# A hybrid decoder layer on one core: low parts of the mixer's weights on VectorE, four more raw weight buffers, and y loaded through GpSimd's queue

## The chip, the core and the metric

The kernel runs on one core of a Trainium2 chip. Its engines work side by side, each through its own instructions in order: TensorE (PE, matmuls; PEld is its loading of weights), VectorE (DVE), ScalarE (ACT), GpSimd (POOL) and SyncE (SP, which here only issues DMA transfers). A transfer is issued by an engine, waits in that engine's order for what it needs, and then lands by itself. The metric is the time of one execution in microseconds of device time, the median of three runs.

## The reference

One layer of a decoder for 512 prompt tokens and 8 samples of 4 tokens, 544 columns in all, with 1024 features in float32:

```python
x = x + 0.5 * SwiGLU_1(RMSNorm(x))          # ffn1: gate and up 1024 x 2816, down 2816 x 1024
z = RMSNorm(x) @ w_in                       # 1024 x 3584, split among the head groups
attn = MoBA(q_a, k_a, v_a)                  # 8 heads of 64, block-sparse attention, paged cache for the samples
rec  = norm(HGRN2(q_b, f_b, i_b)) * silu(g) # 4 heads of 128, gated linear recurrence
x = x + concat(attn, rec) @ w_out           # 1024 x 1024
x = x + 0.5 * SwiGLU_2(RMSNorm(x))          # ffn2, as ffn1
```

It returns the outputs for prompt and samples, the new keys and values, and the states of the recurrence.

## The kernel before

Activations lie transposed: 128 features on the partitions and 544 tokens along the row, worked on in two halves of 272 columns. To come near float32 accuracy each factor is split into a high part (rounded to the short float that a matmul takes at full rate) and a low part (the rest), and each product is three matmuls: high weight with high x, high weight with low x, low weight with high x. The tiles are named so: `whi` and `wlo` are the parts of a weight, `xh` and `xl` those of x.

Three stages follow each other. ffn1 runs until about 402 us, the mixer (w_in, the chains of attention and recurrence, w_out) until about 781 us, ffn2 to the end. A **block** is an output block of 128 features: for w_in (28 blocks) and w_out (8 blocks) it takes two **units** of weights, each 4 x 128 rows by 128 columns (256 KB), and 48 matmuls of 128x272. In the ffn the first NREG = 5 hidden blocks are plain too; from the sixth on the kernel multiplies gate and up in **paired** blocks of seven units, built from five loaded or summed quarters of the weights (a11, a21, their sum, a22, a12), which save a matmul in eight. `xh0..7` and `xl0..7` of the norm's output are the slots that raw weights may use as well once the plain blocks are over; `sq` and `t_g` are copies of partial sums that ScalarE takes out of TensorE's accumulators (`mm` and `sm`) to free them.

Weights pass through two kinds of slots. `w_load` brings a unit from memory into a raw slot (`raw`, four buffers). `w_split` and `split_unit` make the parts in one of six w slots: ScalarE casts `whi`, and then either VectorE subtracts (`wlo = raw - whi`), or ScalarE writes minus the rounded raw into `wlo` in a second pass and GpSimd issues an adding DMA that lays raw onto it (the **transfer**, row `wlo<-raw` of POOL). A raw slot is free when its last reader is done, and that reader is the transfer where there is one. `w_pump` keeps a number of units ahead of TensorE: AHEAD = 4, and AHEAD_MIX = 6 while the job to split is one of the mixer's. Before the change both units of a w_in or w_out block go by transfer; of the ffn's first plain blocks only the second unit does.

The order of all instructions is made by a planner: generators record each instruction with a planned start, computed from costs by shape, and `give_out` (lines 279 to 288) then issues them per engine in the order of planned starts. Nearly every instruction of the profile therefore has line 288, and one goes by tile names. A planned order is fixed: an engine that waits at an instruction holds up whatever is planned behind it.

At the end of the mixer `ffn2` (line 1902) opens its pool on the memory of the mixer's pool, loads the residual `y` (eight tiles of 128 x 544, 272 KB each) from `xspill` (tile name `xs`), and w_out's accumulators are added onto it on VectorE (`y<-mm,y`).

## Time and profile before

| | before |
|---|---|
| runs, us | 1222.38, 1219.51, 1221.71; median 1221.71 |
| profiled execution, us | 1219.56, of which its span 1217.8 |
| PE / PEld busy | 1180.5 (97%) / 1117.7 (92%) |
| DVE / ACT / POOL busy | 780.5 (64%) / 600.8 (49%) / 281.8 (23%) |
| low parts by transfer | 90, 256 KB each, 4.0 us to landing |
| DMA | 177.26 MB, mean 146 GB/s |

The span is what the profile covers; the execution's time is 1.8 us longer. The profile's tables give, for stretches of the span, each engine's busy time, the granted TensorE clock as a share of full speed (PEclk), and the busy share of the DMA engines. In a list of single instructions, the bracket at the end of a line tells how long the engine was idle before it and what ended that.

### The profile page before, as it was taken

To read this page: it belongs to the slowest core of one execution; us is meant where nothing else is said; L and a number is where in the kernel's file an instruction comes from. 1 tells how busy PE (TensorE), PEld (TensorE's weight loads), DVE (VectorE), ACT (ScalarE), POOL (GpSimd) and SP (SyncE) were. 2 spreads that over 40 slices of the span, in tenths; PEclk is the share of its full clock that TensorE was granted. 3 is DMA by queue.
4 is the path that set the end of the run, shared out by engine and by line. 5 is a ranking of instruction groups with operands and counts; after the bars stand their busy time and mean duration, and the time that the engine had idled before them with its cause. 6 is when DMAs were issued, how large, how long until landed. Compare 5 with 4: busy or idle time off the path is not lost.

```text
span 1217.8 us, 26505 instructions
## 1 busy us (share of the span) xinstructions
PE 1180.5 (97%) x10571; PEld 1117.7 (92%) x10571; DVE 780.5 (64%) x1662; ACT 600.8 (49%) x1223; POOL 281.8 (23%) x293
## 2 busy tenths in 40 slices
PE   8999999999999989999999999699989999999998
PEld 8989999999999988889888777599989999999998
DVE  5888458854775377875675357237767478845853
ACT  6645246532555446666556533255544255514642
POOL 4121021101103541213354446141110011101000
PEclk9999999999999989999999999799989999999999
DMA  6566444453325984755787988565455334533232
GB/s 171 130 168 161 127 134 120 124 139 79 87 66 153 223 214 116 174 122 133 225 230 205 277 282 272 124 158 120 118 153 157 86 87 122 142 102 87 53 110 69
DMA packets 234607, 177.26 MB, mean 146 GB/s; under 512 B 14019, under 2 KB 206051, under 8 KB 234484
## 3 DMA queue, kind: packets, MB, share of 16 engines
q1 hardware_dynamic: 206740, 108.83, 30.8%
q0 software_dynamic: 27648, 66.60, 23.8%
q8 instruction: 83, 1.36, 0.5%
q14 instruction: 40, 0.33, 0.1%
q10 hardware_dynamic: 96, 0.14, 0.0%
HBM read 133.94 MB, written 11.83 MB: 120 GB/s over the span
## 4 chain that ended last, share of the span: by engine, by line
PE 85%; DVE 5%; DMA 4%; issue 3%; ACT 1%; POOL 1%; SPq 0%; POOLq 0%; ACTq 0%; DVEq 0%
PE mm L288 58%; PE sm L288 27%; DMA wlo<-raw 1%; DMA raw<-ffn_gate 1%; DMA raw<-w_in 1%; DMA SC<-rsample 0%; DMA xin<-x_prompt 0%; DVE ms_qk L288 0%; DVE wlo L288 0%; DVE xl L288 0%; SPq L288 0%; POOL wlo L288 0%; DVE t_qk L288 0%; ACT sq L288 0%; POOL KV L288 0%
## 5 line engine op out<-in xcount | busy, mean ns | idle before, releaser
L288 PE MATMUL mm<-xh,whi 128*128 128x272 f32 x1216 | 364.5, 300 | 11.1 <-DVE y L288 9.2
L288 PE MATMUL mm<-xl,whi 128*128 128x272 f32 x1216 | 352.6, 290 | 2.0 <-DVE xl L288 1.9
L288 PE MATMUL mm<-xh,wlo 128*128 128x272 f32 x1216 | 352.5, 290 | 0.1
L288 ACT CAST whi<-raw 128x512 fp32r<-128x512 f32 (+1 forms) x256 | 154.5, 606 | 224.5 <-PE mm L288 160.5
L288 PEld LDWEIGHTS mm<-xh,whi 128*128 128x128 f32 x1216 | 231.6, 190 | 26.8 <-issue 13.6
L288 PEld LDWEIGHTS mm<-xl,whi 128*128 128x128 f32 x1216 | 231.3, 190 | 3.1 <-DVE xl L288 3.0
L288 PEld LDWEIGHTS mm<-xh,wlo 128*128 128x128 f32 x1216 | 231.1, 190 | 0.4 <-issue 0.4
L288 DVE TENSOR_TENSOR wlo<-raw,whi 128x512 fp32r<-128x512 f32 (+1 forms) x166 | 113.4, 690 | 61.9 <-ACT whi L288 59.1
L288 PE MATMUL mm<-hw,whi 128*128 128x272 f32 x704 | 132.3, 288 | 0.0
L288 POOL DMA_DIRECT2D wlo<-raw x90 | 81.3, 931 | 218.2 <-ACT wlo L288 181.8
L288 PE MATMUL sm<-xw,whi 128*128 128x272 f32 x648 | 124.3, 290 | 0.4 <-ACT t_g L288 0.4
L288 PE MATMUL mm<-xw,whi 128*128 128x272 f32 x648 | 123.2, 288 | 0.8 <-ACT t_g L288 0.8
L288 PEld LDWEIGHTS mm<-hw,whi 128*128 128x128 f32 x704 | 110.2, 188 | 0.2 <-issue 0.2
L288 PEld LDWEIGHTS sm<-xw,whi 128*128 128x128 f32 x648 | 102.8, 190 | 0.6 <-ACT t_g L288 0.6
L288 PEld LDWEIGHTS mm<-xw,whi 128*128 128x128 f32 x648 | 101.9, 189 | 1.0 <-ACT t_g L288 1.0
L288 PE MATMUL mm<-hw,wlo 128*128 128x272 f32 x352 | 101.2, 287 | 0.0
L288 PE MATMUL sm<-xw,wlo 128*128 128x272 f32 x324 | 94.0, 290 | 0.0
L288 PE MATMUL mm<-xw,wlo 128*128 128x272 f32 x324 | 93.3, 288 | 0.0
L288 PEld LDWEIGHTS mm<-hw,wlo 128*128 128x128 f32 x352 | 66.3, 188 | 0.0
L288 PE MATMUL sm<-xw,xh 128*128 128x272 f32 x304 | 60.6, 295 | 3.0 <-ACT sq L288 3.0
L288 PEld LDWEIGHTS sm<-xw,wlo 128*128 128x128 f32 x324 | 61.7, 190 | 0.2
L288 PE MATMUL mm<-xw,xh 128*128 128x272 f32 x304 | 59.7, 292 | 2.1 <-ACT sq L288 2.1
(324 smaller groups left out, 2163.4 us busy)
## 6 DMA issues: line engine op xcount, KB each, us to landing
wlo<-raw POOLq DMA_DIRECT2D x90, 256.0 KB, 4.0
raw<-ffn_down SPq DMA_DIRECT2D x64, 256.0 KB
raw<-w_in SPq DMA_DIRECT2D x56, 256.0 KB
raw<-ffn_gate SPq DMA_DIRECT2D x38, 256.0 KB
raw<-ffn_up SPq DMA_DIRECT2D x36, 256.0 KB
xl<-ffn_up SPq DMA_DIRECT2D x28, 256.0 KB
xh<-ffn_gate SPq DMA_DIRECT2D x26, 256.0 KB
xh<-ffn_up SPq DMA_DIRECT2D x24, 256.0 KB
```

Of the source, the lines that this page charges most:

```text
L288: call(*map(real, args), **{k: real(v) for k, v in kw.items()})
```

## The change

Of a w_in block only the second unit's low part is now made by a transfer, the first on VectorE; of w_out none is. So 44 of the 90 transfers and as many ScalarE passes go, and VectorE gets 44 subtractions. AHEAD_MIX goes, so four units are kept ahead everywhere. At its start each ffn registers four more raw slots, rawx0 to rawx3, for paired jobs only. The eight loads of y in ffn2 are issued by GpSimd instead of SyncE.

```diff
--- before.py
+++ after.py
@@ -51,8 +51,8 @@
 MIXED = (4, 5, 6, 0, 1, 2, 3, 7)
 OVER, TICK, WARM_COLUMNS = 0.0112, 3.413, 3060
 NREG = 5
+NX = 4
 AHEAD = 4
-AHEAD_MIX = 6
 PACE = 1.1
 WARM = 10
 SLACK = -0.1
@@ -514,12 +514,11 @@
             return [rows[0], rows[1]]
 
         def job(kind, src, nk):
-            out.append({"kind": kind, "src": src, "nk": nk // 2, "raw": [], "done": 0, "paired": kind is not None, "mixer": False})
-
-        def plain(m, nk, r0, c0, mixer=False, start=False):
+            out.append({"kind": kind, "src": src, "nk": nk // 2, "raw": [], "done": 0, "paired": kind is not None})
+
+        def plain(m, nk, r0, c0, transfer=False):
             job(None, quarters(m, nk, r0, c0), nk)
-            out[-1]["mixer"] = mixer
-            out[-1]["start"] = start
+            out[-1]["transfer"] = transfer
 
         def paired(kind, nk, a11, a12, a21, a22, transfer):
             job(kind, [a11, a21, a21 if transfer else None, a22, a12], nk)
@@ -530,8 +529,8 @@
             for g0, ng in FGROUPS[pairs]:
                 for f in range(g0, g0 + ng):
                     if f < NREG:
-                        plain(gate, KD, 0, 128 * f, start=True)
-                        plain(up, KD, 0, 128 * f, start=True)
+                        plain(gate, KD, 0, 128 * f, transfer=True)
+                        plain(up, KD, 0, 128 * f, transfer=True)
                     else:
                         paired("a", KD, *quarters(gate, KD, 0, 128 * f), *quarters(up, KD, 0, 128 * f), pairs)
                 for m in range(0, KD, 2):
@@ -543,9 +542,9 @@
 
         ffn("ffn1", False)
         for n, j in IN_ORDER:
-            plain(a["w_in"][0], KD, 0, COLS[n] + 128 * j, True)
+            plain(a["w_in"][0], KD, 0, COLS[n] + 128 * j, transfer=True)
         for m in range(KD):
-            plain(a["w_out"][0], KD, 0, 128 * m, True)
+            plain(a["w_out"][0], KD, 0, 128 * m)
         ffn("ffn2", False)
         return out
 
@@ -649,7 +648,7 @@
                 job["last"] = self.split_unit(a22, nk, xs[1], job["transfer"])
             drop = {1: (3,), 2: (1,), 4: (2,), 5: (0, 4)}.get(n, ())
         else:
-            self.units.append(self.split_unit(job["raw"][n][0], nk, xs[0], job["mixer"] or n == 1 and job["start"]))
+            self.units.append(self.split_unit(job["raw"][n][0], nk, xs[0], n == 1 and job["transfer"]))
             drop = (n,)
         for i in drop:
             raw, y = job["raw"][i]
@@ -660,11 +659,7 @@
         return True
 
     def w_pump(self):
-        def ahead():
-            mixer = self.splitting < len(self.jobs) and self.jobs[self.splitting]["mixer"]
-            return len(self.units) < (AHEAD_MIX if mixer else AHEAD)
-
-        while (ahead() and self.w_split()) or self.w_load():
+        while (len(self.units) < AHEAD and self.w_split()) or self.w_load():
             pass
 
     def next_w(self, n):
@@ -960,6 +955,7 @@
     def ffn(self, pool, wide, home, x, xg, done, pairs, first=None):
         nc = self.nc
         self.pairs, self.sums, self.hidden_raw = pairs, wide, (pool, "t_h")
+        self.more_slots("a", wide, [f"rawx{i}" for i in range(NX)], [])
         for g0, ng in FGROUPS[pairs]:
             last = g0 + ng == NFF
             hs = []
@@ -1904,7 +1900,7 @@
         with self.pool("ffn2") as pool:
             x = [pool.tile([128, T], F32, name=f"y{k}") for k in range(KD)]
             for k in range(KD):
-                nc.sync.dma_start(x[k], xspill[k])
+                nc.gpsimd.dma_start(x[k], xspill[k])
             xg = []
             for m in range(KD):
```

Where the instructions stand, at three places. First SyncE at the end of w_out, before the change (`raw` are weight buffers, `y<-xs` the residual's loads):

```order
L288 DMA raw_10682<-w_out 128x4x128
L288 DMA raw_10684<-w_out 128x4x128
L288 DMA raw_10686<-w_out 128x4x128
L288 DMA raw_10688<-w_out 128x4x128
L288 DMA y_10694<-xs_57 128x544
L288 DMA y_10696<-xs_58 128x544
L288 DMA y_10698<-xs_59 128x544
L288 DMA y_10700<-xs_60 128x544
L288 DMA y_10702<-xs_61 128x544
L288 DMA y_10704<-xs_62 128x544
L288 DMA y_10706<-xs_63 128x544
L288 DMA y_10708<-xs_64 128x544
```

The same place after the change, still SyncE:

```order
L288 DMA raw_10542<-w_out 128x4x128
L288 DMA raw_10608<-w_out 128x4x128
L288 DMA raw_10626<-w_out 128x4x128
L288 DMA rawx_2092_10646<-ffn_gate 128x4x128
L288 DMA rawx_2093_10648<-ffn_up 128x4x128
L288 DMA rawx_2095_10650<-ffn_up 128x4x128
L288 DMA raw_10671<-w_out 128x4x128
L288 DMA raw_10681<-w_out 128x4x128
L288 DMA raw_10802<-w_out 128x4x128
L288 DMA raw_10809<-w_out 128x4x128
```

The y loads are gone from SyncE, and three loads of ffn2's weights into the new slots stand among those of w_out. On GpSimd at that place before (s is the recurrence's state, sqsum the norm's sum of squares):

```order
L288 TENSOR_TENSOR s_1802_9139<-s_1802_9139,hf_9130 128x512
L288 TENSOR_TENSOR s_1803_9171<-s_1803_9171,hf_9130 128x512
L288 DMA wlo_10634<-raw_10125 128x512
L288 DMA wlo_10651<-raw_10158 128x512
L288 DMA wlo_10674<-raw_10455 128x512
L288 DMA wlo_10679<-raw_10471 128x512
L288 TENSOR_TENSOR sqsum_10731<-sqsum_10731,sq_1923_10745 128x544
```

and after:

```order
L288 TENSOR_TENSOR s_1796_9089<-s_1796_9089,hf_9198 128x512
L288 TENSOR_TENSOR s_1797_9137<-s_1797_9137,hf_9198 128x512
L288 DMA y_10644<-xs_57 128x544
L288 DMA y_10652<-xs_58 128x544
L288 DMA y_10654<-xs_59 128x544
L288 DMA y_10665<-xs_60 128x544
L288 DMA y_10683<-xs_61 128x544
L288 DMA y_10698<-xs_62 128x544
L288 DMA y_10718<-xs_63 128x544
L288 DMA y_10735<-xs_64 128x544
L288 TENSOR_TENSOR sqsum_10710<-sqsum_10710,sq_1917_10737 128x544
```

The four transfers of w_out went and the eight y loads stand where they were.

Second, the first paired block of ffn2. SyncE before, from the loads of that block on (raw are the four raw buffers, xh and xl the norm's slots used for raw weights):

```order
L288 DMA xl_2139_11958<-ffn_up 128x4x128
L288 DMA raw_11960<-ffn_gate 128x4x128
L288 DMA xh_2138_11963<-ffn_gate 128x4x128
L288 DMA xl_2141_11967<-ffn_up 128x4x128
L288 DMA xl_2250_11975<-ffn_gate 128x4x128
L288 DMA xh_2142_11978<-ffn_gate 128x4x128
L288 DMA raw_11994<-ffn_gate 128x4x128
L288 DMA raw_12018<-ffn_down 128x4x128
```

and after:

```order
L288 DMA raw_11731<-ffn_gate 128x4x128
L288 DMA raw_11744<-ffn_gate 128x4x128
L288 DMA raw_11804<-ffn_up 128x4x128
L288 DMA rawx_2127_11878<-ffn_up 128x4x128
L288 DMA rawx_2137_11901<-ffn_gate 128x4x128
L288 DMA xl_2139_11924<-ffn_up 128x4x128
L288 DMA xh_2138_11927<-ffn_gate 128x4x128
L288 DMA xl_2141_11931<-ffn_up 128x4x128
```

The raw loads of this and the next paired block stand ahead of the first xl load. ScalarE in this block before (whi casts for weights, sq and t_g copies out of the accumulators):

```order
L288 CAST whi_12016<-raw_11960 128x512
L288 COPY t_g_12026<-sm_11996 128x272
L288 CAST whi_12035<-raw_11994 128x512
L288 COPY sq_2145_12049<-sm_12014 128x272
L288 CAST whi_12053<-xh_2136_11954 128x512
```

and after:

```order
L288 CAST xh_2130_11977<-t_h_11920 128x544
L288 COPY t_g_11993<-sm_11965 128x272
L288 CAST xh_2166_11999<-rawx_2137_11901 128x512
L288 CAST whi_12011<-rawx_2127_11878 128x512
L288 COPY sq_2145_12020<-sm_11989 128x272
L288 CAST xh_2154_12029<-raw_11731 128x512
```

Ahead of the copy sq stand casts from rawx instead of one from the raw buffer loaded last.

Third, the first paired block of ffn1. SyncE before:

```order
L288 DMA xh_205_1122<-ffn_up 128x4x128
L288 DMA xl_208_1128<-ffn_up 128x4x128
L288 DMA raw_1131<-ffn_gate 128x4x128
L288 DMA xh_207_1133<-ffn_gate 128x4x128
L288 DMA xl_210_1137<-ffn_up 128x4x128
L288 DMA xl_325_1145<-ffn_gate 128x4x128
L288 DMA xh_211_1148<-ffn_gate 128x4x128
L288 DMA pt<-page_table 16x8x1
L288 DMA raw_1167<-ffn_gate 128x4x128
```

and after:

```order
L288 DMA xl_208_1122<-ffn_up 128x4x128
L288 DMA xh_207_1125<-ffn_gate 128x4x128
L288 DMA xl_210_1129<-ffn_up 128x4x128
L288 DMA xl_325_1135<-ffn_gate 128x4x128
L288 DMA xh_211_1138<-ffn_gate 128x4x128
L288 DMA xh_326_1145<-ffn_up 128x4x128
L288 DMA xl_329_1151<-ffn_gate 128x4x128
L288 DMA xh_328_1154<-ffn_up 128x4x128
L288 DMA rawx_196_1160<-ffn_up 128x4x128
```

The load that stood behind the xh and xl loads, raw<-ffn_gate, is replaced there by rawx<-ffn_up. ScalarE before:

```order
L288 CAST whi_1187<-raw_1131 128x512
L288 COPY t_g_1198<-mm_1163 128x272
L288 CAST whi_1207<-raw_1167 128x512
L288 COPY sq_214_1220<-mm_1185 128x272
L288 COPY t_g_1198<-mm_1210 128x272
```

and after:

```order
L288 CAST hw_199_1187<-t_h_1173 128x544
L288 COPY t_g_1201<-mm_1171 128x272
L288 CAST whi_1220<-rawx_196_1160 128x512
L288 COPY sq_214_1233<-mm_1193 128x272
L288 COPY t_g_1201<-mm_1217 128x272
```

In both a weight's cast stands directly ahead of the copy sq, before from raw, after from rawx.

## Rows read from the trace of the kernel before

**Rows 1.** The page's busy times (share of the span, instructions), and its chain of work that ended last, by engine.

```profile
PE 1180.5 (97%) x10571; PEld 1117.7 (92%) x10571; DVE 780.5 (64%) x1662; ACT 600.8 (49%) x1223; POOL 281.8 (23%) x293
...
PE 85%; DVE 5%; DMA 4%; issue 3%; ACT 1%; POOL 1%; SPq 0%; POOLq 0%; ACTq 0%; DVEq 0%
```

**Rows 2.** What TensorE waited for over the whole span: total us, number of waits, longest.

```profile
PE mm L288 <- DVE y L288: 9.2, 1, 9.2
PE sm L288 <- ACT sq L288: 3.0, 1, 3.0
PE sm L288 <- DVE kt L288: 2.8, 2, 2.5
...
PE mm L288 <- ACT sq L288: 2.1, 1, 2.1
```

**Rows 3.** Stretches around the start of ffn2: from:to, width, busy us (instructions) of PE, PEld, DVE, ACT, POOL, then PEclk, DMA share, GB/s.

```profile
771.30:778.30 7.00, 7.00 (x57) 7.00 (x57) 0.00 (x0) 3.19 (x6) 1.87 (x2) 1.00 0.23 42
778.30:781.30 3.00, 2.97 (x24) 2.75 (x22) 0.00 (x0) 1.31 (x3) 1.73 (x2) 1.00 0.93 195
781.30:790.40 9.10, 0.00 (x0) 0.00 (x0) 0.47 (x2) 0.00 (x0) 0.00 (x0) 0.70 0.87 223
790.40:794.00 3.60, 3.58 (x16) 3.58 (x17) 1.84 (x5) 2.12 (x4) 0.00 (x0) 0.50 0.97 320
794.00:797.00 3.00, 3.00 (x21) 3.00 (x21) 1.53 (x3) 1.75 (x4) 1.40 (x1) 0.80 0.26 95
```

**Rows 4.** The same table for the first paired block of ffn2.

```profile
893.00:895.50 2.50, 2.08 (x13) 1.60 (x12) 1.64 (x3) 0.49 (x2) 0.00 (x0) 1.00 1.10 324
895.50:898.50 3.00, 0.01 (x2) 0.00 (x1) 0.31 (x1) 0.96 (x3) 0.90 (x1) 0.85 0.77 229
898.50:905.00 6.50, 5.99 (x25) 5.67 (x26) 4.95 (x5) 2.60 (x7) 3.41 (x4) 0.50 0.54 76
905.00:908.00 3.00, 3.00 (x15) 3.00 (x15) 2.44 (x5) 2.47 (x5) 0.00 (x0) 0.53 0.71 188
```

**Rows 5.** The same table for the first paired block of ffn1.

```profile
86.50:88.40 1.90, 0.01 (x1) 0.01 (x1) 0.31 (x1) 0.96 (x3) 0.87 (x1) 1.00 0.81 229
88.40:92.00 3.60, 3.45 (x15) 3.13 (x15) 3.60 (x3) 2.59 (x6) 3.01 (x4) 0.53 0.42 77
```

**Rows 6.** GpSimd's instructions one by one at the start of ffn2: start, duration, what.

```profile
779.35 1.73 POOL L288 DMA_DIRECT2D wlo<-raw  x2 [1.85 <-ACT whi L288]
```

**Rows 7.** The chain that ended last, in order of time (start, us, what), at the start of ffn2.

```profile
779.90 5.25 DMA wlo<-raw
```

**Rows 8.** SyncE's queue at the start of ffn2: start, us, what.

```profile
778.50 7.08 SPq L288 DMA_DIRECT2D raw<-w_out  x4
785.87 4.25 SPq L288 DMA_DIRECT2D y<-xs  x8
```

**Rows 9.** VectorE's instructions at the start of ffn2.

```profile
770.38 0.72 DVE L288 TENSOR_TENSOR xl<-rec,xh 128x544 fp32r<-128x544 f32 x1
789.93 0.79 DVE L288 TENSOR_TENSOR y<-mm,y 128x272 f32<-128x272 f32 x2 [18.83 <-DMA y<-xs]
```

**Rows 10.** The instructions on the tile wlo: duration in ns, minimum/median/maximum, and first and last start; the last line is the transfers' time from issue to landing.

```profile
L288 DVE TENSOR_TENSOR wlo<-raw,whi x166: 557/684/1692, 8.9 to 1198.1; 128x512 fp32r<-128x512 f32 x134, 128x384 fp32r<-128x384 f32 x32
L288 ACT ACTIVATE wlo<-raw x90: 613/627/645, 21.4 to 873.3; 128x512 fp32r<-128x512 f32 x90
L288 POOL DMA_DIRECT2D wlo<-raw x90: 851/874/1502, 25.3 to 874.2; - x90
...
DMA to landing us min/median/max: 3.1/4.0/7.9
```

**Rows 11.** ScalarE's instructions in the first paired block of ffn2.

```profile
897.54 0.62 ACT L288 CAST whi<-raw 128x512 fp32r<-128x512 f32 x1 [4.05 <-DMA raw<-ffn_gate]
898.07 0.38 ACT L288 COPY sq<-sm 128x272 f32<-128x272 f32 x1
```

**Rows 12.** SyncE's queue ahead of that block.

```profile
886.02 0.37 SPq L288 DMA_DIRECT2D xh<-ffn_up  x1
...
891.87 1.81 SPq L288 DMA_DIRECT2D raw<-ffn_gate  x1
```

**Rows 13.** ScalarE's instructions in the first paired block of ffn1.

```profile
87.44 0.62 ACT L288 CAST whi<-raw 128x512 fp32r<-128x512 f32 x1 [3.17 <-DMA raw<-ffn_gate]
87.96 0.38 ACT L288 COPY sq<-mm 128x272 f32<-128x272 f32 x1
```

**Rows 14.** SyncE's queue ahead of that block.

```profile
81.75 0.59 SPq L288 DMA_DIRECT2D xh<-ffn_gate  x1
...
83.40 0.55 SPq L288 DMA_DIRECT2D raw<-ffn_gate  x1
```

**Rows 15.** The table of stretches in the mixer: two of seven that make up 402 to 757 us with the sum of all seven, and one around the wait for kt.

```profile
402.00:450.00 48.00, 43.39 (x525) 41.15 (x524) 29.08 (x88) 19.35 (x38) 26.85 (x35) 0.97 0.96 233
...
500.00:550.00 50.00, 49.25 (x357) 40.74 (x356) 39.82 (x109) 30.97 (x77) 8.50 (x9) 1.00 0.55 128
...
sum 355.00, PE 347.28 PEld 292.89 DVE 229.83 ACT 196.19 POOL 147.09; mean PE 49.61 PEld 41.84 DVE 32.83 ACT 28.03 POOL 21.01
...
446.00:454.00 8.00, 6.81 (x36) 6.33 (x37) 6.22 (x16) 4.84 (x9) 2.54 (x3) 0.57 0.55 132
```

**Rows 16.** The page's costliest groups: ScalarE's casts of weights, count, busy us, mean ns, and the idle time before them.

```profile
L288 ACT CAST whi<-raw 128x512 fp32r<-128x512 f32 (+1 forms) x256 | 154.5, 606 | 224.5 <-PE mm L288 160.5
```

## The prediction

> **What bounds the kernel now.** I read the page's list of busy times and its chain first. TensorE is busy 97% of the span and takes 85% of the chain [rows 1], so a saving on VectorE, ScalarE or GpSimd is worth time only where TensorE waits for it. Next came the list of what TensorE waited for. It is short and top-heavy: one wait of 9.2 us for a VectorE addition into y, one of 3.0 and one of 2.1 for ScalarE's copy of a partial sum (sq), and some small ones with kt at their head [rows 2]. I then cut the span into stretches around the three long ones, because a stall costs twice here: after each the granted clock stands near 0.5. A matmul at full clock takes 7.00/57 = 0.123 us, at half clock 3.58/16 = 0.224 us [rows 3].
>
> Start of ffn2: idle 781.3 to 790.4, 9.10 us; then 16 matmuls at half clock cost 3.58 - 16 x 0.123 = 1.6 us too much, and the next 21 another 0.4 [rows 3]. Together **11.1 us**.
>
> First paired block of ffn2 (888 to 908): idle 0.42 + 2.99 + 0.51 (widths minus busy time); 25 matmuls in 5.99 us are 2.9 too long, 15 in 3.00 us 1.2 [rows 4]. Together **8.0 us**.
>
> First paired block of ffn1: idle 1.89 + 0.15, and 15 matmuls in 3.45 us, 1.6 too long [rows 5]. Together **3.6 us**.
>
> **The y loads.** Their chain in the trace of before: the last low-part transfer of w_out is issued by GpSimd at 779.35 [rows 6] and lands 5.25 us after 779.90 [rows 7]. SyncE's row of four w_out loads stands from 778.50 for 7.08 us, since each load writes a raw slot that such a transfer still reads. Behind it, in the same queue, the eight y loads go out from 785.87 to 790.1 [rows 8], and VectorE's first addition starts at 789.93 after 18.83 us without work, ended by y's landing [rows 9]. Yet the last reader of the memory that y takes over, VectorE's xl<-rec, ended at 770.38 + 0.72 = 771.1 [rows 9]. From 771.1 to 785.87 y waits in a queue, not for memory.
>
> The change takes all three links out: GpSimd issues y; no w_out unit goes by transfer, so GpSimd has no low-part DMA ahead of them (the order has two s products and then y0 to y7); and SyncE's w_out loads wait for a VectorE subtraction instead of a landing. With 0.87 us for an issue and 4.0 us to land, both medians of the low-part DMAs [rows 10], y0 lands at about 771.1 + 0.9 + 4.0 = 776 and y7, seven issues later, near 782. TensorE needs the first addition at 781.3. VectorE's order has some subtractions ahead of it at 0.684 each [rows 10]; it was idle from 771.3 to 781.3 [rows 3], so I put the addition at about 780 and the stall at nothing. If four subtractions more stand in the way it is some 2 us. Gain **11.1, bounds 8 to 11.1**; nothing up to 4 if y is late (rival 2).
>
> A rule against this edit: the Trainium skill, "SBUF — State Buffer", section "SBUF: two separate sides", says that a DMA issued from GpSimd can be starved of descriptors while VectorE holds the port pair that the two share. The longest low-part issue here took 1.50 us against a median of 0.87, and the longest VectorE subtraction 1.69 against 0.684 [rows 10], which fits such blocking without proving it. With 1.5 us for each issue y0 lands at 776.6 and y7 at 787, still ahead of its own block, so the sum is the same by either; only a blockage of several us for y0 would matter, and that is rival 2.
>
> **The four extra raw slots in ffn2.** TensorE's 2.99 us wait is for the copy sq at 898.07. ScalarE executes in order, and ahead of the copy stands a cast of a gate weight (897.54) that had waited 4.05 us for its load [rows 11]. SyncE issued that load at 891.87, behind the xh and xl loads that begin at 886.02 [rows 12]; it landed 897.54 - 891.87 = 5.7 us later. After the change the load has a slot of its own, and the order shows all raw loads of this block and the next ahead of the first xl load; if the xl and xh loads keep their time these go out by 886.02 instead of 891.87. Even at 5.7 us they land by 891.7; TensorE's wait for sq began at 895.5 [rows 4], so nothing is late. Gain **8.0, bounds 1.4 to 8.0**; the low bound is what the same edit gives in ffn1.
>
> **The extra slots in ffn1.** The same picture: the cast at 87.44 waits 3.17 us for its load, and the copy sq at 87.96 follows [rows 13]; the load was issued at 83.40 [rows 14]. Here the new order is worse: one load of the second block (rawx, from ffn_up) still stands behind eight xl and xh loads, and ScalarE's cast of it is again the row just before the copy. It loses two or three places, so it goes out when the load of 81.75 did [rows 14], 1.4 to 1.6 us earlier, and the rest of the stall and its half clock stay. Gain **1.4, bounds 0 to 3.6**.
>
> **w_in and w_out.** 28 units of w_in and 16 of w_out move their low part from ScalarE (0.627), GpSimd's issue (0.87) and a 4.0 us transfer to one VectorE subtraction of 0.684 [rows 10]. VectorE gets 28 x 0.684 = 19.2 us in w_in, where it is busy 229.8 of 355 us (65%, then 70%), and 16 x 0.684 = 10.9 in w_out. ScalarE loses 44 x 0.627 = 27.6, GpSimd 44 x 0.87 = 38, and 44 transfers leave the DMA engines, whose share is 0.96 from 402 to 450 [rows 15]. TensorE waits for no weight there: it is busy 347.3 of 355 [rows 15], and the named waits are chain results [rows 2]. So the subtractions lie under matmuls. Where one stands ahead of the kt chain (the new order has one before its reductions) it adds 0.7 to a 2.5 us stall that is followed by half clock (36 matmuls in 6.81 us from 446 to 454, 2.4 too long [rows 15]); fewer transfers in the crowded stretch before it may take as much away. I take **0, bounds -6 to +5** (all of that stall away; or four such delays and their clock).
>
> **Four units ahead.** A block's 48 matmuls take 48 x 0.123 = 5.9 us, so four units are two blocks, nearly 12 us; the second unit's low part needs a cast of 0.61 [rows 16], 0.63 + 0.87 and a landing of 4.0, 6.1 at the median, and 10 at the longest landing of 7.9 [rows 10]. It is prepared last, with some 7.5 us left. Only landings above 5.4 us are late, by up to 2.5 us; that is inside the bound above.
>
> **Sum.** -11.1 - 8.0 - 1.4 + 0 = -20.5 us against the profiled execution's own 1219.56 us (span 1217.8 and 1.8 around it): 1199.1. That execution is 2.2 us under the median of 1221.71, so for a median I say **1200**; with the small terms' bounds, 1196 to 1206.
>
> **Rivals.**
> 1. *All stalls go* (0.10). ffn1's block closes too and the relieved DMA engines shorten the kt wait: 3.6 instead of 1.4 and up to 3 in the mix, about 1195. For it: DMA share 0.96. Against: the cast ahead of sq in ffn1.
> 2. *y is late on GpSimd's queue* (0.13). If y0 lands at 785 instead of 776, TensorE idles about 4.3 us from 781.3 and pays 2.0 for the clock: 4.8 gained, not 11.1. About 1206 to 1207. The skill's rule above would act through this. Against: VectorE and GpSimd have little work there [rows 3].
> 3. *The stall moves in ffn2* (0.07). A rawx load is held by its slot's last reader, and the xl and xh loads are now queued behind it on SyncE: 8.0 becomes about 1: 1207.
> 4. *VectorE becomes the bound in the mix* (0.20 in all). Each subtraction standing ahead of a chain operation delays TensorE by 0.684; all 44 exposed cost 30.1: 1221.7 - 20.5 + 30.1 = 1231, slower. It decides when 30 of 44 are exposed (20.5 us); a change above 0.3% (3.7 us, about what a measurement tells) needs 36. For it: VectorE at 39.8 of 50 us from 500 to 550 [rows 15]. Against: TensorE is busy 49.25 there. Exposed in part (8 to 16) it gives 1206 to 1212: 0.08; enough for no difference 0.05; slower 0.07.
>
> **Numbers.** The forecast has 0.50, the rivals as given; faster is 0.50 + 0.10 + 0.13 + 0.07 + 0.08 = 0.88, same 0.05, slower 0.07. Range 1194 to 1213: it holds the forecast, rivals 2 and 3, and rival 4 in part.
>
> **What would show it.** Right: VectorE's first addition into y by 781 and no TensorE gap near 781; y landing from 776; the wait for sq in ffn2 under 0.5 us at full clock; in ffn1 still one of about 2 us; VectorE near 70% from 402 to 757 with no wait of TensorE for wlo. Wrong: a GpSimd issue held beyond 778; a ScalarE cast from rawx waiting before an sq copy in ffn2; new TensorE waits in the mix above 10 us in sum.

## The result and the profile after

The changed kernel took 1207.56 us (median of four runs, 1205.87 to 1210.64) beside 1222.05 for the kernel before on the same chip: a ratio of 0.9886, 95% interval 0.9856 to 0.9916, 14.5 us less. The forecast was 1200, its range 1194 to 1213. The direction and the range held; a third of the gain was missing.

The page's busy times after (engines: busy us, share of the span, instructions):

```profile
PE 1171.9 (97%) x10571; PEld 1109.2 (92%) x10571; DVE 808.4 (67%) x1706; ACT 579.3 (48%) x1179; POOL 246.0 (20%) x257
```

TensorE stays the bound at 97%, VectorE rose from 64% to 67%. What TensorE waited for over the whole span (us in total, times, longest):

```profile
PE sm L288 <- issue: 4.3, 12, 0.5
PE mm L288 <- DVE xl L288: 3.4, 5, 1.6
PE sm L288 <- DMA KV<-cache_v,idx: 3.0, 2, 1.5
PE mm L288 <- DVE t_h L288: 2.5, 2, 1.3
...
PE mm L288 <- ACT sq L288: 2.3, 1, 2.3
...
PE mm L288 <- DVE wlo L288: 1.5, 1, 1.5
...
PE sm L288 <- DVE kt L288: 0.5, 1, 0.5
```

Against [rows 2] the 9.2 us for y and the 3.0 us for sq in ffn2 are gone, and kt fell from 2.8 to 0.5. The 2.1 us for sq in ffn1 became 2.3. New are a wait for wlo (1.5), two for t_h (2.5) and twelve pauses of together 4.3 us that nothing in the profile releases ("issue").

At the start of ffn2 (from:to, width, busy us (instructions) of PE, PEld, DVE, ACT, POOL, then PEclk, DMA share, GB/s):

```profile
770.00:779.00 9.00, 8.10 (x51) 7.22 (x50) 6.67 (x14) 2.73 (x5) 0.00 (x0) 0.89 0.31 89
779.00:785.00 6.00, 6.00 (x50) 6.00 (x49) 2.69 (x5) 2.48 (x4) 4.33 (x8) 1.00 0.61 192
785.00:791.00 6.00, 6.00 (x50) 6.00 (x50) 4.37 (x9) 3.34 (x6) 1.19 (x1) 1.00 1.05 365
```

TensorE is busy throughout from 779, where [rows 3] has 9.10 us with nothing. GpSimd's queue there (start, us, what, idle before and what ended it):

```profile
780.16 4.33 POOL L288 DMA_DIRECT2D y<-xs  x8 [21.41 <-PE mm L288]
```

VectorE's instructions there, the mixer's last and the first of ffn2:

```profile
778.82 0.72 DVE L288 TENSOR_TENSOR xl<-rec,xh 128x544 fp32r<-128x544 f32 x1
...
785.53 0.78 DVE L288 TENSOR_TENSOR y<-mm,y 128x272 f32<-128x272 f32 x2
```

The mixer's last reader ends at 778.82 + 0.72 = 779.5, not 771.1, since in this trace the tail of the mixer lies some 8 us later; GpSimd issues y at 780.16, 0.54 us each. The bracket says that a TensorE matmul ended its wait, about 0.3 us after VectorE's last read. VectorE adds the first halves at 785.53. TensorE needed them no earlier: its own work had moved with the tail.

The first paired block of ffn2 lies at 880 to 891 now, in the same table:

```profile
880.00:890.00 10.00, 10.00 (x82) 10.00 (x81) 6.70 (x11) 6.20 (x13) 3.04 (x3) 1.00 0.99 259
890.00:896.00 6.00, 6.00 (x51) 6.00 (x50) 5.38 (x9) 4.16 (x8) 4.16 (x3) 1.00 1.02 249
```

No idle time and full clock, where [rows 4] has 3.9 us idle and half clock. The casts ahead of sq found their loads landed, as ScalarE's instructions show:

```profile
885.33 0.62 ACT L288 CAST whi<-rawx 128x512 fp32r<-128x512 f32 x1
886.64 0.39 ACT L288 COPY sq<-sm 128x272 f32<-128x272 f32 x1 [0.69 <-DVE sm L288]
```

SyncE's queue ahead of them:

```profile
876.84 0.37 SPq L288 DMA_DIRECT2D rawx<-ffn_up  x1
878.33 0.37 SPq L288 DMA_DIRECT2D rawx<-ffn_gate  x1
880.27 0.37 SPq L288 DMA_DIRECT2D xl<-ffn_up  x1
```

The rawx loads went out at 876.84 and 878.33, ahead of the first xl load at 880.27; the copy sq waits only for the VectorE operation ahead of it, 0.69 us.

**Where the time went, by position.** TensorE executes the same 7656 matmuls of 272 columns in both kernels. The table gives, for the start of the same matmul counted from the first, how much later (+) or earlier (-) than in the trace of before it comes. In the mixer the order of blocks against chains differs, so a single column inside it may be off by several us; from 798 us on the columns are comparable. Rows are the traces of the changed kernel, of its repeats and of the experiments below; each is one execution, and a trace can lie several us from the median of its kernel (rawx_ffn2_again's is the fastest of six, win_both's the slowest of four).

```
us in the trace of before   48.8    78.9   106.5   376.5   765.2   798.2   828.2   890.9   908.3  1191.4
changed, first result       +0.5    +2.3    +4.2    +3.7    +8.2    -5.5    -5.4    -5.6   -14.4   -14.0
changed, set 2              +0.9    +2.8    +3.9    +3.4    +6.3    -7.3    -7.3    -7.5   -16.3   -15.7
changed, set 3              +0.6    +2.5    +5.1    +4.6    -0.8   -14.4   -14.4   -14.6   -23.4   -23.1
y_back_sp                   +0.8    +2.5    +3.5    +3.1    -2.1   -15.7   -15.7   -15.7   -24.5   -24.3
y_back_sp_again             +1.2    +3.2    +4.2    +3.8    +4.1    -9.4    -9.4    -9.4   -18.3   -18.0
rawx_ffn2                   +0.0    +0.0    +2.2    +2.2    -0.9   -14.5   -14.5   -14.7   -23.5   -23.2
rawx_ffn2_again             +0.1    +0.1    +1.2    +1.4    -4.4   -18.0   -18.0   -18.2   -27.0   -26.6
no_rawx                     +0.7    +0.7    +1.2    +1.2    -2.2   -15.8   -15.8   -16.0   -16.2   -16.2
hold_sum                    -0.3    -0.3    +2.4    +2.4    +3.9    -9.7    -9.7    -9.9   -18.7   -18.2
hold_all                    -0.2    +0.9    -2.2    +3.8   +10.7    -2.9    -2.9    -3.0   -11.8   -11.4
win_both                    +0.2    +1.7    +2.8    +2.4    +6.9    -5.7    -5.7    -5.9   -14.7   -14.4
wout_both                   +0.5    +2.2    +3.1    +2.7    +0.6   -11.4    -7.5    -7.8   -16.7   -16.3
y_pool_alone                +0.6    +0.6    +2.7    +2.7    +7.0    +2.7    +3.6    +3.4    +1.3    +1.5
```

For the first result: 3.7 us lost in ffn1, 9.2 gained over the mixer and the start of ffn2, 8.8 gained between 890.9 and 908.3 and nothing after. The forecast had -1.4, -11.1 and -8.0. What is missing lies in ffn1 and in the mixer.

### The profile page after: what moved, and what is told of

Same layout as the page of the kernel before. It is cut to its first block, busy times and chain, and to the rows that moved or that the text cites. A ratio compares the mean times of both kernels' runs of the same rounds, so it can differ in the third digit from the quotient of the medians.

```text
span 1204.1 us, 26396 instructions
## 1 busy us (share of the span) xinstructions
PE 1171.9 (97%) x10571; PEld 1109.2 (92%) x10571; DVE 808.4 (67%) x1706; ACT 579.3 (48%) x1179; POOL 246.0 (20%) x257
## 4 chain that ended last, share of the span: by engine, by line
PE 85%; DVE 5%; DMA 4%; ACT 3%; issue 2%; POOL 1%; SPq 0%; ACTq 0%; POOLq 0%; DVEq 0%
PE mm L288 58%; PE sm L288 27%; DMA rawx<-ffn_up 1%; DMA wlo<-raw 1%; DVE wlo L288 1%; DMA xl<-ffn_up 1%; DVE xl L288 1%; DMA KV<-cache_v,idx 1%; ACT xh L288 1%; ACT sq L288 1%; ACT whi L288 0%; DMA xin<-x_prompt 0%; POOL sqsum L288 0%; DVE ms_qk L288 0%; DVE raw L288 0%
## 5 line engine op out<-in xcount | busy, mean ns | idle before, releaser
L288 ACT CAST whi<-raw 128x512 fp32r<-128x512 f32 (+1 forms) x242 | 145.9, 605 | 225.1 <-PE mm L288 173.3
L288 DVE TENSOR_TENSOR wlo<-raw,whi 128x512 fp32r<-128x512 f32 (+1 forms) x196 | 136.7, 703 | 72.5 <-ACT whi L288 69.9
L288 POOL DMA_DIRECT2D wlo<-raw x46 | 41.7, 923 | 178.1 <-ACT wlo L288 127.4
L288 PEld LDWEIGHTS mm<-xw,wlo 128*128 128x128 f32 x324 | 61.0, 188 | 0.1
```

What stands on the lines that cost most here:

```text
L288: call(*map(real, args), **{k: real(v) for k, v in kw.items()})
```

## The experiments

Twelve runs in three sets, each set on one chip with its own runs of the kernel before. Only within a set are times compared; why, the second set shows.

| set | kernel | median us | ratio to before, 95% interval |
|---|---|---|---|
| 1 (before 1220.92) | rawx_ffn2 | 1195.25 | 0.9790 (0.9756 to 0.9824) |
| 1 | no_rawx | 1204.09 | 0.9857 (0.9818 to 0.9896) |
| 1 | y_back_sp | 1197.65 | 0.9813 (0.9775 to 0.9850) |
| 1 | y_pool_alone | 1219.38 | 0.9988 (0.9953 to 1.0024) |
| 2 (before 1222.40) | changed (after_again) | 1205.30 | 0.9872 (0.9847 to 0.9896) |
| 2 | y_back_sp_again | 1206.59 | 0.9892 (0.9862 to 0.9922) |
| 2 | hold_sum | 1202.21 | 0.9841 (0.9810 to 0.9873) |
| 2 | hold_all | 1207.55 | 0.9876 (0.9843 to 0.9909) |
| 3 (before 1219.58) | changed (after_third) | 1197.01 | 0.9821 (0.9797 to 0.9845) |
| 3 | rawx_ffn2_again | 1198.41 | 0.9828 (0.9805 to 0.9851) |
| 3 | win_both | 1203.02 | 0.9861 (0.9833 to 0.9889) |
| 3 | wout_both | 1203.15 | 0.9864 (0.9836 to 0.9892) |

### What the extra slots do in ffn1

What went wrong there is seen in the changed kernel's trace near 50 us. TensorE's wait:

```profile
51.21 0.40 PE L288 MATMUL mm<-xh,wlo 128*128 128x272 f32 x1 [1.54 <-DVE wlo L288]
```

GpSimd ahead of it:

```profile
38.20 1.30 POOL L288 TENSOR_TENSOR rawx<-rawx,rawx 128x512 f32<-128x512 f32 x1 [10.63 <-DMA rawx<-ffn_up]
39.79 0.87 POOL L288 DMA_DIRECT2D rawx<-rawx  x1 [0.30 <-POOL rawx L288]
40.38 2.07 POOL L288 DMA_DIRECT2D wlo<-raw  x2
```

SyncE's queue, the early loads and the raw load that came late:

```profile
31.99 0.45 SPq L288 DMA_DIRECT2D rawx<-ffn_gate  x1
32.49 1.05 SPq L288 DMA_DIRECT2D rawx<-ffn_up  x2
...
44.90 0.38 SPq L288 DMA_DIRECT2D raw<-ffn_gate  x1
```

ScalarE's cast of that load:

```profile
47.78 0.62 ACT L288 CAST whi<-raw 128x512 fp32r<-128x512 f32 x1 [3.75 <-DMA raw<-ffn_gate]
```

VectorE behind it:

```profile
49.28 0.44 DVE L288 TENSOR_TENSOR xw<-hw,xw 128x272 fp32r<-128x272 f32 x1 [3.02 <-ACT xw L288]
...
50.47 0.68 DVE L288 TENSOR_TENSOR wlo<-raw,whi 128x512 fp32r<-128x512 f32 x1
```

With the new slots the first paired block's quarters are loaded at 32 us, though TensorE reaches that block only near 80. GpSimd's sum of two of them (rawx2) then has an early place too, in front of two low-part transfers: GpSimd stands 10.63 us for the loads to land, and the transfers go out at 40.38, where the kernel before issued the first at 34.74. Behind that transfer a raw slot comes free late, SyncE's next load goes out at 44.90 (38.02 before), ScalarE's cast waits 3.75 us for it, a cast of xw and VectorE stand behind, and TensorE waits 1.54 us for a low part at 51.21.

**rawx_ffn2**, the slots in ffn2 alone:

```diff
-        self.more_slots("a", wide, [f"rawx{i}" for i in range(NX)], [])
+        if first is None:
+            self.more_slots("a", wide, [f"rawx{i}" for i in range(NX)], [])
```

> The changed kernel with the four extra raw slots registered in ffn2 alone. Theory 1 (in ffn1 the slots hurt: GpSimd's sum of two early loads stands ahead of low-part transfers, and the first paired blocks stall anew): the 4.2 us that the first 120 us lose go, so about 1203, TensorE's wait for wlo near 50 us is gone, the waits for t_h near 84 and 96 us too, and ffn2 keeps its gain. Rival (the early loss has another cause in the change): within 1 us of the changed kernel.

> The changed kernel with the extra slots in ffn2 alone, beside the changed kernel. Theory 1: no wait for wlo near 50 us, 2 to 4 us less than the changed kernel, all of it before 120 us. Rival (the 10 us between this kernel and the changed one on different chips were the edit's): 8 to 12 us less.

The wait near 50 us is gone in both traces: from 48.8 to 78.9 us they lose nothing, the changed kernel 1.8 to 1.9 us in each of its three. At 376.5 us they stand at +2.2 and +1.4, the changed kernel at +3.4 to +4.6. But 1.1 to 2.2 us are lost in the first paired block even here, where the engines have the order of the kernel before up to about 388 us: that stall is not the same in each execution, and the profile of before was among its shorter ones. In time the difference on one chip is not to be seen: 1198.41 against 1197.01 with intervals that overlap, where 2 to 4 us less was expected.

All traces together tell more than these two. Seven have the slots in ffn1 as the changed kernel has them; five do not (before, rawx_ffn2 and its repeat, no_rawx, y_pool_alone), and their order in ffn1 is the same. At 78.9 us the seven stand at +1.7 to +3.2, the five at 0 to +0.7. From there to 106.5 us the seven lose 0.9 to 2.6 us (mean 1.4) and the five 0 to 2.2 (mean 1.2). So the edit's own loss in ffn1 is about 2 us, it arises before 78.9 us, and the first paired block comes out even. The 12 us between set 1 and the first result were not this edit's.

**hold_sum** and **hold_all**. The planner gets a floor for GpSimd's sums in ffn1 (hold_sum), and for the loads into extra slots too (hold_all, to which alone the second piece belongs); `held` is set in ffn1 alone, and the floor is put back after each load:

```diff
+    def hold(self):
+        if self.held:
+            self.order.floor = max(self.order.floor, self.order.free["pe"])
...
+        if x["extra"] is not None:
+            self.hold()
...
         if job["src"][i] is None:
+            self.hold()
             self.nc.gpsimd.tensor_tensor(raw_k, parts[0], parts[1], op=ALU.add)
...
         if job["paired"] and i == 3:
+            self.hold()
             self.nc.gpsimd.dma_start(parts[1], raw_k, accum_op=ALU.add)
```

> The changed kernel, but in ffn1 GpSimd's sums of the quarters (the add into rawx2 and the adding transfer after it) are planned no earlier than TensorE's place at which they are recorded, so that they stand behind five low-part transfers instead of ahead of them; the three early rawx loads stay at 32 us. Theory 1 (the sum on GpSimd's queue is what cost): the wait for wlo near 50 us is gone, 1.8 us less than the changed kernel; the stalls of the first paired block stay. Rival (the early loads' own traffic): the wait stays.

> As the run with the sums held, and in ffn1 the loads into extra slots are held too, so they go out near 55 us, and the second job's load that the copy sq stands behind comes after two xh and xl loads, not eight. Theory 1: no wait for wlo near 50 us, the wait for sq in the first paired block shrinks from 2.3 us to under 1, and ffn1 ends 3 to 5 us earlier than in the changed kernel. Rival (the transition is bound by the loads' bandwidth whatever their order): the wait for sq stays at 2 us or moves to the second block, gain under 2.

hold_sum keeps the early loads and the wait is gone: nothing lost from 48.8 to 78.9 us, against 1.9 in the changed kernel on this chip, while the three early rawx loads still go out at 31.6 to 33.1 us. So GpSimd's order cost it, not the loads' traffic. The stall of the first paired block stayed, as foreseen (2.7 us). hold_all shortened the first paired block as expected (from +0.9 to -2.2 between 78.9 and 106.5 us): with six of the xh and xl loads out of the way, the load behind which sq stands lands in time. It then lost 6.0 us by 376.5, most of it between 160 and 180 us at the second group of blocks, so ffn1 ended no earlier than in the changed kernel (+3.8 against +3.4), where 3 to 5 us earlier was expected. That the loads held back came late there is a reading of the order, not tried apart.

### What the y loads needed

**y_back_sp**, y on SyncE again in the changed kernel, and **y_pool_alone**, y on GpSimd in the kernel before, are the same line each way:

```diff
-                nc.gpsimd.dma_start(x[k], xspill[k])
+                nc.sync.dma_start(x[k], xspill[k])
```

> The changed kernel with the y loads back on SyncE. Theory 2 (what held y were w_out's transfers, through the raw slots; the queue itself is not the point): the order now has y ahead of the last w_out loads on SyncE, so no wait for y and within 1.5 us of the changed kernel. Rival (GpSimd's queue is what freed y): a wait of 5 to 9 us for y, 1214 to 1218.

> The kernel before with nothing changed but the y loads on GpSimd. Theory 2: y stands behind w_out's last low-part transfer on GpSimd, which ends near 781.1, so y lands near 785 instead of 789.9; TensorE still idles 4 us and pays half clock: gain 4 to 5, about 1217. Rival (the queue is the point): the whole 11 us, about 1211.

> The changed kernel with y on SyncE once more, beside the changed kernel on the same chip. Theory 3: equal to it within 2 us. Rival: 8 to 10 us faster, 1196 to 1200.

With y on SyncE and no w_out transfers TensorE has no wait for y either, and beside the changed kernel on one chip the two are equal within what a measurement tells: 1206.59 and 1205.30. In set 1 it gave 1197.65, far from the first result's 1207.56 where 1.5 us was expected; that difference goes with the set, as shown further on. With y on GpSimd and the transfers kept, y stands behind them in GpSimd's queue (the trace of y_pool_alone):

```profile
785.46 1.74 POOL L288 DMA_DIRECT2D wlo<-raw  x2 [1.85 <-ACT whi L288]
786.79 4.22 POOL L288 DMA_DIRECT2D y<-xs  x7
```

What TensorE waits for there, same kernel:

```profile
PE mm L288 <- DVE y L288: 7.1, 2, 6.6
```

The wait is 6.6 us instead of 9.2, longer than the 4 us expected, and between the columns 765.2 and 798.2 it gains 4.3 us, as expected. ffn1 and the mixer had lost 7.0 us by 765.2 (longer waits for kt and hqh among it), so its time is not told from that of before.

**wout_both**, both units of a w_out block by transfer again:

```diff
-            plain(a["w_out"][0], KD, 0, 128 * m)
+            plain(a["w_out"][0], KD, 0, 128 * m, transfer=2)
...
-            self.units.append(self.split_unit(job["raw"][n][0], nk, xs[0], n == 1 and job["transfer"]))
+            self.units.append(self.split_unit(job["raw"][n][0], nk, xs[0], job["transfer"] == 2 or n == 1 and job["transfer"]))
```

> The changed kernel, but both units of each w_out block by transfer again. Two transfers now stand ahead of y on GpSimd and others right behind y7. Theory 2: no wait for y above 1 us, since the two are issued early with only four units ahead, but a new wait of 1 to 4 us for a low part that stands behind the eight y loads. Rival (any w_out transfer holds y): TensorE waits 5 us or more for y again.

TensorE's waits from 765 to 910 us in wout_both:

```profile
PE mm L288 <- DMA wlo<-raw: 2.0, 1, 2.0
PE mm L288 <- DVE y L288: 1.4, 1, 1.4
```

The wait for y is 1.4 us where none above 1 was expected, and the wait of 2.0 for a low part issued behind y7 came as expected, with a lower granted clock after it (0.80 from 795 to 800 us). So the rival's 5 us did not come. The time is 1203.15 against 1197.01, and all but one of the changed kernel's six runs lie below all four of wout_both. From 765.2 to 828.2 us its trace gains 8.1 us where the changed kernel's gains 13.6: some 5.5 us of the y step hang on the w_out edit. Another part lies just before: TensorE waits 5.6 us for xl at 759.5 instead of 2.0, where GpSimd's two products for s stand behind a w_out transfer (754.80 us instead of 747.63) and VectorE's small operation beside them took 2.77 us.

With y on GpSimd and the w_out transfers kept, six units ahead (y_pool_alone) leave a wait of 6.6 us for y and four (wout_both) one of 1.4; in the first four transfers stand ahead of y, in the second two. So AHEAD_MIX is a likely part of what freed y, but the two kernels also differ in w_in and the slots, and no run changes AHEAD_MIX alone. What is shown is that y on either queue is free once w_out's transfers are gone and four units are kept ahead.

### What the slots do in ffn2

**no_rawx**, the changed kernel without that one line:

```diff
-        self.more_slots("a", wide, [f"rawx{i}" for i in range(NX)], [])
```

> The changed kernel without the extra raw slots at all. Theory 1: ffn1 gains 4.2 us back and ffn2's first paired block loses 8.0 to 8.5 again, with the 3 us wait for sq and half clock after it: about 1212. Rival (it is the four units ahead, or fewer transfers, that closed that wait): 1203, no such wait.

TensorE's waits from 765 to 910 us in no_rawx:

```profile
PE sm L288 <- ACT sq L288: 2.2, 1, 2.2
```

The wait for sq is back, and from 890.9 to 908.3 us it gains 0.2 us where each kernel with the slots gains 8.8 to 8.9. Its 1204.09 is the rival's number, not the 1212 expected, but the rival had no such wait; the whole set ran some 10 us below what was expected of it, and against rawx_ffn2 beside it, which differs in the slots of ffn2 alone, it is 8.8 us slower, as foreseen. The stall that is closed has a spread too: y_pool_alone, without the slots, gains 2.1 us there.

### What w_in's edit does

**win_both**, both units of a w_in block by transfer, four units ahead: the plain job of w_in gets transfer=2, with the same line in w_split as in wout_both.

> The changed kernel, but both units of each w_in block by transfer again (four units ahead stay). Theory 4 (28 subtractions on VectorE lie under matmuls, the 28 transfers as well): within 2 us of the changed kernel. Rival (VectorE's subtractions delay the chains of the mixer): 5 to 10 us faster than the changed kernel between 402 and 757 us; second rival (the transfers delayed chains through ScalarE, GpSimd and the DMA engines): 5 to 10 us slower there.

TensorE's wait for kt in the mixer (402 to 765 us) in win_both:

```profile
PE sm L288 <- DVE kt L288: 5.2, 2, 4.7
```

The same in the changed kernel on the same chip:

```profile
PE sm L288 <- DVE kt L288: 0.5, 1, 0.5
```

With the transfers kept the wait for kt is 4.7 us at its longest; with the first unit on VectorE 0.5. The stretch around it in win_both (columns as above):

```profile
440.00:450.00 10.00, 6.47 (x64) 6.04 (x62) 3.61 (x14) 5.33 (x12) 6.83 (x8) 0.98 0.94 233
450.00:460.00 10.00, 8.79 (x44) 6.99 (x45) 8.13 (x23) 7.86 (x15) 2.68 (x3) 0.68 0.82 215
```

The same stretch in the changed kernel:

```profile
440.00:450.00 10.00, 10.00 (x98) 9.37 (x97) 9.18 (x25) 6.48 (x14) 3.55 (x3) 1.00 0.43 110
450.00:460.00 10.00, 8.79 (x59) 7.31 (x57) 8.45 (x25) 8.28 (x18) 0.89 (x1) 1.00 0.46 115
```

win_both has TensorE busy 6.47 of 10 us and then a granted clock of 0.68, at a DMA share of 0.94; the changed kernel is busy throughout in the first of the two stretches, at 0.43, and keeps its clock in the second. In time it is 1203.02 against 1197.01, and none of its four runs is as fast as any of the changed kernel's six (1201.49 at the least, 1201.31 at the most). So theory 4 falls and the second rival holds: the 28 transfers delayed the chains, and w_in's edit is worth about 6 us.

The chain that ended last in win_both shows the way that the delay took (start, us, what):

```profile
422.46 5.41 DMA wlo<-raw
...
427.92 9.78 DMA raw<-w_in
...
437.78 0.62 ACT whi L288
...
439.23 0.90 POOL wlo L288
...
445.11 1.11 POOL at L288
...
450.47 0.60 DVE kt L288
```

A load of w_in goes out only when the transfer ahead of it in the chain has landed, and its own landing takes 9.78 us in this crowded stretch. ScalarE's cast waits for it, GpSimd's next transfer waits for ScalarE, and behind that transfer stand GpSimd's cache loads and its sum `at`, for which ScalarE, VectorE and the kt chain wait in turn. In the changed kernel on the same chip GpSimd makes that sum at 439.90 instead of 445.08, and the chain from 425 to 447 us lies almost all on VectorE. The wait for kt goes with the transfers in all traces: 2.5 to 4.7 us at the longest in the three kernels that make the first units of w_in by transfer (before, y_pool_alone, win_both), at six units ahead and at four, and 0.7 at most in the others. How much of the delay each link carries was not tried apart.

### The same kernel in several sets

> The changed kernel itself, on one chip with the next three. From 428 to 750 us its trace and that of the kernel with y on SyncE have the same TensorE order, and yet it is some 8 us longer, partly in pauses of TensorE of 0.4 to 0.5 us that nothing in the profile releases. Theory 3 (these belong to the executions of that one chip or loading, not to the edit): 1196 to 1201 here, within 2 us of the kernel with y on SyncE. Rival (y on GpSimd costs the mixer 8 to 10 us): 1205 to 1210 again.

> The changed kernel as a control for the three beside it on the same chip: 1197 to 1207, since the kernel with y on SyncE, its near twin, has given 1197.7 on one chip and 1206.6 on another.

The changed kernel gave 1207.56 (first result), 1205.30 (set 2) and 1197.01 (set 3), and its near twin with y on SyncE 1197.65 and 1206.59, while the kernel before stayed at 1219.6 to 1222.4. Theory 3 was right in that the two are equal on one chip and wrong in the level: the twin came up to the changed kernel, not the changed kernel down to the twin. With set 3, where the changed kernel too is at 1197, the 8 to 10 us go with the set and not with the queue of y. The traces show where: at runs of small matmuls in the mixer. TensorE's instructions at one such place in the changed kernel, first result:

```profile
428.80 0.47 PE L288 MATMUL sm<-sqsum,hk 128*32 128x32 f32 x33
...
429.61 0.33 PE L288 MATMUL sm<-hqh,hk 128*32 128x16 f32 x12 [0.23 <-issue]
430.42 0.26 PE L288 MATMUL sm<-hqh,hk 128*32 128x16 f32 x6 [0.47 <-issue]
431.17 0.29 PE L288 MATMUL sm<-hqh,hk 128*32 128x16 f32 x5 [0.50 <-issue]
```

The same place of the same order in y_back_sp:

```profile
428.23 0.47 PE L288 MATMUL sm<-sqsum,hk 128*32 128x32 f32 x33
...
428.54 0.52 PE L288 MATMUL sm<-hqh,hk 128*32 128x16 f32 x33
```

In the one, the 33 matmuls sm<-hqh,hk go out in pieces with pauses of 0.23 to 0.50 us that nothing in the profile ends; in the other they go out at once. Over the whole span these pauses sum to 3.5 to 6.7 us in the first result and in all four kernels of set 2, and to at most 1.3 in the eight others. From 376.5 to 765.2 us the changed kernel loses 4.5 us in the first result and gains 5.4 in set 3, by the same instructions. The pauses are 3.4 of these 10 us (4.3 against 0.9). Most of the rest lies at the same places: counted by TensorE's instructions, the first result falls 2.8 us behind set 3 from 427.5 to 432 us, where its pauses sum to 1.7, and 4.2 us from 730 to 752, where they sum to 1.5; from 432 to 575 us it loses nothing. What makes TensorE pause is left open too: the profile names no releaser, and chip and loading of the program could not be told apart here. The kernel before has no such pause in its one trace, and its time hardly moved between the sets, so whether the change makes a kernel open to them is not shown either.

## Why the prediction was right, and where it was not

**y loads, forecast 11.1.** Right in what was gained, in part wrong in why. The wait and the half clock after it are gone; from 765.2 to 798.2 us the traces of the changed kernel gain 13.6 to 13.7, 2.5 more than forecast; the mixer's tail, whose order changed too, lies in that stretch, and its part was not tried apart. y0 went out at 780.16 instead of the 771 to 772 that I worked with, and the first addition came at 785.53, not by 781, since the mixer's tail moved; that cost nothing because TensorE's need moved with it. The weight that I gave to GpSimd's queue was wrong: SyncE does as well with w_out's transfers gone and four units ahead. And I looked at four units ahead only as a danger for low parts, not as a way to have fewer transfers ahead of y.

The port rule of the Trainium skill, "SBUF — State Buffer", section "SBUF: two separate sides", decided nothing here: the eight issues took 4.33 us together while VectorE was busy 2.69 of 6 us. Whether VectorE held the shared ports in that time no run shows. The prediction's hint for it was misread: the subtraction of 1.69 us in [rows 10] is the one at 13.96 us, beside a sum on GpSimd from 13.51 to 15.10, with no transfer issued by GpSimd in that time.

**Slots in ffn2, forecast 8.0.** Right, mechanism and size: 8.8 us in the first result, 8.8 to 8.9 in every kernel of the sets that has the slots, all against the one trace of before.

**Slots in ffn1, forecast a gain of 1.4, bounds 0 to 3.6.** Wrong, and outside the bounds: a loss of 3.7 in the first result, of which about 2 are the edit's. The step that failed is the one that followed a single queue. I read SyncE's and ScalarE's order around 80 us and never asked what else the early loads trigger: the sum on GpSimd at 38 us, ahead of low-part transfers that ffn1's plain blocks need. That is worth about 2 us (hold_sum). And in this trace the wait for sq did not shrink (2.3 us): the xl and xh loads themselves began at 78.58, not 76.44, and the load behind them went out at 84.56, later than the old one at 83.40 [rows 14]. ScalarE's cast and copy there:

```profile
90.14 0.62 ACT L288 CAST whi<-rawx 128x512 fp32r<-128x512 f32 x1 [4.89 <-DMA rawx<-ffn_up]
90.67 0.38 ACT L288 COPY sq<-mm 128x272 f32<-128x272 f32 x1
```

The loads on SyncE's queue:

```profile
78.58 0.37 SPq L288 DMA_DIRECT2D xl<-ffn_up  x1
...
84.56 0.56 SPq L288 DMA_DIRECT2D rawx<-ffn_up  x1
```

One trace misleads here. Over all traces the wait for sq is 0.4 to 2.5 us with the slots (seven, mean 1.3) and 1.8 to 3.0 without (five, mean 2.3), so it did shrink, by about 1 us. But each of the seven has a wait or two of 1.2 to 1.3 us for t_h that none of the five has, which the prediction did not contain, and the block as a whole came out even. The rest of the 3.7 us is the block's own spread.

**w_in and w_out, forecast 0, bounds -6 to +5.** The time was hidden as forecast: VectorE is busy 245.12 of 355 us, 69%, with no wait of TensorE for wlo in the mixer; the whole stretch in the table of stretches:

```profile
402.00:757.00 355.00, 345.93 (x3977) 292.41 (x3977) 245.12 (x665) 177.99 (x415) 117.86 (x129) 1.00 0.63 181
```

But 0 was mis-sized. I named the kt wait and the crowded DMA stretch and let the two ends cancel; win_both shows that the relief wins, by about 6 us, the far end of my bounds. The half of rival 1 that has the kt wait shortened came true. In the first result the mixer's slower execution, with 4.3 us of pauses, hid that (+4.5 us), an effect that the prediction did not contain; it goes with the set, and what part the change has in it is open. The w_out edit, which I put at 0 here, is worth another 6 us (wout_both), most of it counted above in the y step.

**Sum.** Forecast -20.5; the traces give -14.0 (first result), -15.7 (set 2) and -23.1 (set 3). By its own working the sum is 1221.71 - 20.5 = 1201.2 for a median, not 1200. The range of 1194 to 1213 held all three medians, in part by luck: the terms missed in opposite ways (ffn1 by some 3 us of the edit's, the y step by 2.5, the mixer by 4 to 5 either way), and the set decided which of them won. Of the rivals, none was the cause: y was not late, ffn2's stall did not move on, VectorE did not become the bound, and ffn1's block did not close.

No kernel here beats the changed one beyond what a measurement tells. The slots in ffn2 alone are 3.5 us shorter by the trace and 1.4 longer by the median on the same chip; hold_sum is 3.1 us below the changed kernel in the one set that has it; its four runs (1200.45 to 1203.33) all lie below the other's six (1204.24 to 1208.45), but the intervals of the two ratios overlap.

## What to carry to other kernels

A resource that lets work start earlier moves everything that the planner ties to it: read the order of each engine around the new early place, not only around the stall that it should close. Where a transfer is the last reader of a buffer, the queue that loads the next buffer waits for its landing, and whatever stands behind it in that queue waits too; moving y alone did not free it, and taking the transfers away and keeping fewer units ahead did, on either queue. And put a control of the changed kernel into each set: on these chips the same kernel differed by 10 us while the kernel before did not show it.

## What the runs showed of the hardware

Four things that I had not expected. TensorE pauses of 0.2 to 0.9 us inside runs of small matmuls, most of them 128x16, 10 to 15 of them in five of the traces and at most one (up to 1.3 us) in the others, with the same instructions or nearly so. GpSimd's issue of a plain load took 0.54 us (y), against 0.87 at the median for an adding transfer. And a stall's size is itself a spread: the first paired block of ffn1, in one and the same order, lost 0.5 to 2.2 us more in four other traces (from 78.9 to 106.5 us: rawx_ffn2 and its repeat, no_rawx, y_pool_alone) than in the trace that the prediction was made from. Last, VectorE slows beside GpSimd's own arithmetic: in each of the 14 traces 26 to 31 VectorE operations take over 0.4 us more than the median of their kind, 22 to 27 us in all, and all but one or two of them overlap one of the 101 operations that GpSimd computes itself. In wout_both the operation that took 2.77 us at 754.42 takes 0.17 elsewhere in the same chain; GpSimd multiplied from 754.80 to 757.16. No experiment moved GpSimd's arithmetic to test this.
